# Packet sizes and issue times of loads and stores in a DMA-bound weight-normalised matmul

## The chip, the cores and the metric

The kernel runs on one core of one Trainium2 chip. The metric is the device time of one execution in microseconds (us), lower is better, as the median of several executions. The span of a profile is about 1.3 us shorter than the time measured for the same execution.

## The reference

```
W_adapted = W + scale * (lora_A @ lora_B)                  # 256 x 256
W_final   = W_adapted / sqrt(sum(W_adapted ** 2, axis=0) + 1e-8) * m
y         = x.reshape(-1, 256) @ W_final                   # x: 32768 x 256, float32
```

The weights are tiny. What counts is that x (33.6 MB) is read once and y (33.6 MB) is written once.

## The kernel before

x is cut into 8 blocks of 4 MB. Each block has 8 chunks, and each chunk is 4 rows of 1 KB on each of 128 partitions. The kernel keeps 5 blocks in the on-chip memory, and the results overwrite x in place. Blocks 0 to 2 must be stored before blocks 5 to 7 can be loaded. SP, an engine that here only issues transfers, issues the loads (queue q1 in the profile), and ACT, one of the compute engines, the stores (q10).

```
    loads = [(0, 2), (2, 2), (4, CH - 4)] + units[1 : XBUFS - 1]      # (first chunk, chunks)
    loads += [((XBUFS - 1) * CH, CH - 3)]
    loads += [(XBUFS * CH - 3 + c, 1) for c in range(3)] + units[XBUFS:]
    ...
    stores = [(b * CH, CH, 21 + b) for b in range(F - 1)]             # (..., issue after chunk)
    stores += [(G - CH, CH // 2, 24), (G - CH // 2, CH // 2, 24)]
    FIRST = len(stores)
    stores += [(G + c, 1, G + 3) for c in range(4)]
    stores += [(G + 4, CH - 4, 47)]
    stores += [(b * CH, CH, max(47, (b + 1) * CH - 1)) for b in range(F + 1, NBLK - 1)]
    stores += [(g0, cnt, g0 + cnt - 1) for g0, cnt in units[-2:]]
    HALF = FIRST - 2
    ...
        if loads[n][0] == XBUFS * CH:          # block 5 waits for blocks 0, 1 and half of 2
            for k in range(HALF + 1):
                nc.sync.wait_ge(sem(f"store{k}"), 16)
```

Here CH = 8 (chunks in a block), F = 3 and G = 24. One transfer of n rows per partition leaves 128 packets of n KB in the trace, which is 8 on each of the 16 DMA engines. The size of a transfer in rows is therefore also its packet size. The rest of a chunk's way is a cast to bf16 on POOL, transposes on PE (the matrix engine), a copy on VectorE, the product on PE, and a copy back on ACT.

Of the kernel before, what the change touches and what calls it, by code (L numbers as in the profile page):

```python
# [11 lines left out]
def kernel(  # L12
# [10 lines left out]
    nc = tc.nc  # L23
# [6 lines left out]
    x_flat = x.flatten_outer_dims()  # L30
    out_flat = out.flatten_outer_dims()
# [4 lines left out]
    J = 4  # L36
    DJ = 32
    BLK = DJ * P
    NBLK = N // BLK
# [3 lines left out]
    XBUFS = 5  # L43
    CH = DJ // J
    NCH = NBLK * CH

    NPR = NCH // 2
# [1 line left out]
    NXB = 2  # L49

    REST = 15
    IDLE = 8
    NXT = 2
    F8 = 2 * J * P

# [7 lines left out]
    def sb(name, shape, dtype):  # L63
        return ctx.enter_context(nc.sbuf_tensor(name, shape, dtype))
# [4 lines left out]
    x_bufs = [sb(f"x_sb{k}", [P, DJ, IN], FP32) for k in range(XBUFS)]  # L69
    xb_bufs = [sb(f"xb{k}", [P, 2 * J, IN], BF16) for k in range(NXB)]  # L70
# [4 lines left out]
    m_row = sb("m_row", [1, OUT], FP32)  # L75
    identity = sb("identity", [P, P], FP32)
    zeros = sb("zeros", [P, P], FP32)
    ones = sb("ones", [P, P], FP32)
# [18 lines left out]
    mb_ps = y_ps[1][:, 2, :]  # L97
# [3 lines left out]

    units = [(b * CH, CH) for b in range(NBLK - 1)]
    units += [(NCH - CH, CH // 2), (NCH - CH // 2, CH // 2)]
    loads = [(0, 2), (2, 2), (4, CH - 4)] + units[1 : XBUFS - 1]


    loads += [((XBUFS - 1) * CH, CH - 3)]
    loads += [(XBUFS * CH - 3 + c, 1) for c in range(3)] + units[XBUFS:]
    load_of = {g: n for n, (g0, cnt) in enumerate(loads) for g in range(g0, g0 + cnt)}




    F = NBLK - XBUFS
    G = F * CH
    stores = [(b * CH, CH, 21 + b) for b in range(F - 1)]
    stores += [(G - CH, CH // 2, 24), (G - CH // 2, CH // 2, 24)]
    FIRST = len(stores)
    stores += [(G + c, 1, G + 3) for c in range(4)]
    stores += [(G + 4, CH - 4, 47)]  # L120
    stores += [(b * CH, CH, max(47, (b + 1) * CH - 1)) for b in range(F + 1, NBLK - 1)]
    stores += [(g0, cnt, g0 + cnt - 1) for g0, cnt in units[-2:]]
    HALF = FIRST - 2


    late = [nc.alloc_semaphore(f"store{n}") for n in range(FIRST, len(stores))]
    sems = {f"store{FIRST + k}": s for k, s in enumerate(late)}

    def sem(name):
        if name not in sems:  # L130
            sems[name] = tc.alloc_semaphore(name)
        return sems[name]

    def in_sbuf(g0, cnt):
        b, c = divmod(g0, CH)
        return x_bufs[b % XBUFS][:, c * J : (c + cnt) * J, :]

    def in_dram(dram, g0, cnt):
        (u0, ucnt), = [u for u in units if u[0] <= g0 < u[0] + u[1]]
        unit = dram[u0 * J * P : (u0 + ucnt) * J * P].rearrange("(p j) k -> p j k", p=P)  # L140
        return unit[:, (g0 - u0) * J : (g0 - u0 + cnt) * J, :]

    def load_x(n):
        nc.sync.dma_start(
            out=in_sbuf(*loads[n]), in_=in_dram(x_flat, *loads[n])
        ).then_inc(sem(f"load{n}"), 16)

    def store_y(n):
        nc.scalar.dma_start(
            out=in_dram(out_flat, *stores[n][:2]), in_=in_sbuf(*stores[n][:2])  # L150
        ).then_inc(sem(f"store{n}"), 16)


    nc.sync.dma_start(
        out=w_nat[:], in_=W.rearrange("(p t) o -> p t o", t=KC)
    ).then_inc(sem("load_w"), 16)
    nc.scalar.dma_start(
        out=a_nat[:], in_=lora_A.rearrange("(p t) r -> p t r", t=KC)
# [1 line left out]
    nc.scalar.dma_start(out=b_nat[:], in_=lora_B).then_inc(sem("load_b"), 16)  # L160
    nc.scalar.dma_start(out=m_row[:], in_=m[None, :]).then_inc(sem("load_m"), 16)
    for n in range(len(loads)):
        if loads[n][0] == XBUFS * CH:


            for k in range(HALF + 1):
                nc.sync.wait_ge(sem(f"store{k}"), 16)
        if loads[n] == units[-1]:
            nc.sync.wait_ge(sem(f"store{HALF + 1}"), 16)
        load_x(n)  # L170


# [3 lines left out]
        out=identity[:],  # L176
        in_=zeros[:],
# [3 lines left out]
        pattern=[[-1, P]],  # L181
        channel_multiplier=1,
    ).then_inc(sem("ident"), 1)
    for p in range(NPR):
        b, c = divmod(p, PRB)
        for g in (2 * p, 2 * p + 1):
            if g == 0 or load_of[g - 1] != load_of[g]:
                nc.gpsimd.wait_ge(sem(f"load{load_of[g]}"), 16)
        if p == 0:


            nc.gpsimd.wait_ge(sem("dve"), 4)
        if p == REST:
            nc.gpsimd.wait_ge(sem(f"store{HALF}"), 16)
        if p >= NXB:
            nc.gpsimd.wait_ge(sem("turned"), p - NXB + 1)
        nc.gpsimd.tensor_copy(  # L197
            out=xb_bufs[p % NXB][:],
            in_=x_bufs[b % XBUFS][:, 2 * c * J : 2 * (c + 1) * J, :],
        ).then_inc(sem("rounded"), 1)  # L200

    nc.gpsimd.wait_ge(sem("turned"), NPR - NXB + 1)
    nc.gpsimd.memset(xb_bufs[NPR % NXB][:], 0.0).then_inc(sem("rounded"), 1)  # L203


    for _ in range(IDLE):
        nc.gpsimd.wait_ge(sem("ident"), 1)


    dv = sem("dve")  # L210
    nc.vector.memset(ones[:], 1.0)
# [8 lines left out]
        out=wa[:], in0=ab_ps, scalar=float(scale), in1=w_nat[:], op0=ALU.mult, op1=ALU.add  # L220
    ).then_inc(dv, 1)
    nc.vector.wait_ge(dv, 3)
    nc.vector.tensor_mul(out=sq[:], in0=wa[:], in1=wa[:]).then_inc(dv, 1)  # L223
    nc.vector.wait_ge(sem("pe"), 4)
    nc.vector.tensor_copy(out=m_all[:], in_=mb_ps).then_inc(dv, 1)  # L225
    nc.vector.wait_ge(dv, 5)
    for t in range(KC):
# [5 lines left out]
    for t in range(KC):  # L233
        i = nc.vector.tensor_mul(out=w_final[:, t], in0=wam[:, t], in1=rnorm[:])  # L234
    i.then_inc(dv, 1)
    for p in range(NPR):
        nc.vector.wait_ge(sem("turned"), p + 1)
        nc.vector.tensor_copy(  # L238
            out=xt_bufs[p % NXT][:].rearrange("p r t -> p (r t)").bitcast(FP32),
            in_=xt_ps[p % 2][:],  # L240
        ).then_inc(sem("copied"), 1)


    nc.scalar.wait_ge(dv, 1)

    nc.scalar.activation(out=warm[:], in_=eps_col[:], func=AF.Sqrt)  # L246
    nc.scalar.wait_ge(sem("pe"), 3)
    nc.scalar.activation(  # L248
        out=norm[:], in_=n2_ps, func=AF.Sqrt, bias=eps_col[:]
    ).then_inc(sem("act"), 1)  # L250
    drains = 0
    for g in range(NCH):
        b, c = divmod(g, CH)
        nc.scalar.wait_ge(sem("product"), g + 1)

        nc.scalar.copy(  # L256
            out=x_bufs[b % XBUFS][:, c * J : (c + 1) * J, :], in_=y_ps[g % 2][:]
        ).then_inc(sem("room"), 1)
        due = [n for n in range(len(stores)) if stores[n][2] == g]
        if due:  # L260
            drains += 1
            nc.scalar.drain().then_inc(sem("done"), 1)  # L262
            nc.scalar.wait_ge(sem("done"), drains)
            for n in due:
                store_y(n)


    pe = sem("pe")
# [6 lines left out]
    for t in range(KC):  # L275
        i = nc.tensor.matmul(  # L276
            ab_ps[:, t, :], aT[:, t * P : (t + 1) * P], b_bf[:], start=True, stop=True
        )
    i.then_inc(pe, 1)
    nc.tensor.wait_ge(dv, 4)  # L280

    for t in range(KC):
# [1 line left out]
            n2_ps, ones[:], sq[:, t, :], start=(t == 0), stop=(t == KC - 1)  # L284
        )
    i.then_inc(pe, 1)
    nc.tensor.wait_ge(sem("load_m"), 16)
    nc.tensor.matmul(mb_ps, ones[0:1, :], m_row[:], start=True, stop=True).then_inc(pe, 1)  # L288
    def take(name):

        nc.tensor.sem_inc(sem(name), -1).wait_op(sem(name), 1, "sem-ge")  # L291
# [4 lines left out]
        j_order.append(a + J // 2)  # L296

    def turned(p):
        take("rounded")

        for j in range(2 * J):
            i = nc.tensor.transpose(  # L302
                xt_ps[p % 2][:, j * P : (j + 1) * P],
                xb_bufs[p % NXB][:, j, :].bitcast(FP32),
                identity[:],
            )
        i.then_inc(sem("turned"), 1)

    def product(p):
        take("copied")  # L310
        for h in range(2):
            take("room")
            for t in range(KC):
                for j in j_order:
                    r = (h * J + j) * P
                    i = nc.tensor.matmul(  # L316
                        y_ps[h][:, j, :],
                        xt_bufs[p % NXT][:, r : r + P, t],
                        w_final[:, t, :],
                        start=(t == 0 and (j % (J // 2)) == 0),  # L320
                        stop=(t == KC - 1 and (j % (J // 2)) == (J // 2) - 1),
                    )
            i.then_inc(sem("product"), 1)

    turned(0)

    nc.tensor.wait_ge(dv, 8)
    nc.tensor.sem_inc(sem("room"), 2)
    with nc.Fori(0, NPR // 2, 1, engines=[PE], head_slot={PE: 128}):
        turned(1)  # L330
        product(0)
        turned(0)
        product(1)

# [1 line left out]
    critical.close()  # L336
    tc.close()
    tc.compile()
    for s in late:
        nc.sync.wait_ge(s, 16)  # L340
        nc.sync.sem_clear(s)


# [33 lines left out]
```

## Time and profile before

| | before |
|---|---|
| median time, 3 executions | 162.48 us (162.4 to 162.73) |
| span of the profile | 161.3 us |
| bytes moved | 67.42 MB, 418 GB/s over the span |
| PE busy | 59% |
| last store issued | 132.23 us |

The DMA engines are busy from the second of the 40 slices to the last but one, so the bytes set the time. The question for any change is how much engine time is wasted. The prediction shows the lines.

The trace has a record of each DMA packet with its queue, bytes, start and duration. **Time lost up to t** is t minus (bytes moved by then) / 432.2 GB/s. That is the rate of 16 engines with 32 KB packets at their median of 1213 ns, and about what the trace holds for long (430 to 433). While the engines run at that rate, the number stands still. Where it grows, engine time is being wasted.

### The profile page before, as it was taken

To read this page: it belongs to the slowest core of one execution; us is meant where nothing else is said; L and a number is where in the kernel's file an instruction comes from. 1 tells how busy PE (TensorE), PEld (TensorE's weight loads), DVE (VectorE), ACT (ScalarE), POOL (GpSimd) and SP (SyncE) were. 2 spreads that over 40 slices of the span, in tenths; PEclk is the share of its full clock that TensorE was granted. 3 is DMA by queue.
4 is the path that set the end of the run, shared out by engine and by line. 5 is a ranking of instruction groups with operands and counts; after the bars stand their busy time and mean duration, and the time that the engine had idled before them with its cause. 6 is when DMAs were issued, how large, how long until landed. Compare 5 with 4: busy or idle time off the path is not lost. (4 is left out here: it accounts for less than half of the span.)

```text
span 161.3 us, 2012 instructions
## 1 busy us (share of the span) xinstructions
PE 95.2 (59%) x786; PEld 83.8 (52%) x786; DVE 46.6 (29%) x44; ACT 63.9 (40%) x67; POOL 62.9 (39%) x39
## 2 busy tenths in 40 slices
PE   0491899999999700000199999999999940000000
PEld 0160799999998600000179989989899930000000
DVE  0439635353635300000033535353445300000000
ACT  3010076868686520000027675856776850000000
POOL 1085339776764000000674479198676200000000
PEclk9999999999999995555559999999999998555555
DMA  4999999999899999989999999999999999999995
GB/s 163 427 455 459 390 504 406 390 488 423 374 412 361 511 423 390 473 374 451 427 482 414 386 463 421 407 433 433 422 484 419 406 479 414 400 479 423 386 443 228
DMA packets 4356, 67.42 MB, mean 418 GB/s; under 512 B 625, under 2 KB 642, under 8 KB 1666
## 3 DMA queue, kind: packets, MB, share of 16 engines
q1 hardware_dynamic: 2160, 33.82, 49.5%
q10 hardware_dynamic: 2194, 33.59, 48.7%
q14 instruction: 2, 0.02, 0.0%
HBM read 33.85 MB, written 33.55 MB: 418 GB/s over the span
## 5 line engine op out<-in xcount | busy, mean ns | idle before, releaser
L256 ACT COPY x_sb<-y_ps 128x1024 f32<-128x1024 f32 x64 | 62.0, 1014 | 60.0 <-PE y_ps L316 57.8
L197 POOL CAST xb<-x_sb 128x2048 bf16<-128x2048 f32 x32 | 60.4, 1900 | 61.3 <-DMA out_dram<-x_sb 27.7
L316 PE MATMUL y_ps<-w_final,xt 128*128 128x256 bf16 x512 | 63.6, 278 | 1.2 <-PEq L291 1.1
L238 DVE COPY xt<-xt_ps 128x1024 f32<-128x1024 f32 x32 | 39.2, 1224 | 72.6 <-PE xt_ps L302 72.6
L316 PEld LDWEIGHTS y_ps<-w_final,xt 128*128 128x128 bf16 x512 | 51.1, 100 | 8.5 <-issue 1.9
L302 PE MATMUL xt_ps<-identity,xb 128*128 128x128 f32 x264 | 37.0, 287 | 28.2 <-PEq L291 28.2
L302 PEld LDWEIGHTS xt_ps<-identity,xb 128*128 128x128 f32 x264 | 31.7, 148 | 30.3 <-issue 30.0
L283 PE MATMUL y_ps<-sq,ones 128*128 128x256 f32 x4 | 2.1, 674 | 1.6 <-DVE sq L223 1.6
L272 PE MATMUL y_ps<-identity,a_nat 128*16 128x128 f32 x2 | 0.6, 394 | 4.1 <-DMA a_nat<-in_lora_A_dram 4.1
L248 ACT ACTIVATE norm<-y_ps,eps_col 128x256 f32<-128x256 f32 x1 | 0.5, 473 | 5.8 <-PE y_ps L283 5.8
L234 DVE TENSOR_TENSOR w_final<-wam,rnorm 128x256 bf16<-128x256 f32 x2 | 2.5, 1266 | 0.0
L283 PEld LDWEIGHTS y_ps<-sq,ones 128*128 128x128 f32 x4 | 1.2, 326 | 2.3 <-DVE sq L223 2.1
L272 PEld LDWEIGHTS y_ps<-identity,a_nat 128*16 128x16 f32 x2 | 0.1, 88 | 4.1 <-issue 4.1
L246 ACT ACT_TABLE_LOAD x1 | 1.3, 1283 | 2.4 <-issue 2.4
L203 POOL MEMSET xb<- 128x2048 bf16 x1 | 1.8, 1804 | 0.7 <-PE xt_ps L302 0.7
L231 DVE RECIPROCAL rnorm<-norm 128x256 f32<-128x256 f32 x1 | 1.7, 1747 | 0.0
L225 DVE COPY m_all<-y_ps 128x256 f32<-128x256 f32 x1 | 0.4, 424 | 3.3 <-PE y_ps L288 3.3
L214 DVE CAST b_bf<-b_nat 16x256 bf16<-16x256 f32 x1 | 0.3, 281 | 3.5 <-DMA b_nat<-in_lora_B_dram 3.5
L288 PE MATMUL y_ps<-m_row,ones 1*128 1x256 f32 x2 | 1.2, 706 | 0.0
L276 PE MATMUL y_ps<-b_bf,aT 16*128 16x256 bf16 x2 | 0.6, 404 | 0.7 <-DVE aT L216 0.7
L219 DVE SCALAR_TENSOR_TENSOR wa<-y_ps,w_nat 128x512 f32<-128x512 f32 x1 | 0.7, 692 | 0.8 <-PE y_ps L276 0.8
L288 PEld LDWEIGHTS y_ps<-m_row,ones 1*128 1x128 f32 x2 | 0.5, 308 | 0.6 <-issue 0.6
(13 smaller groups left out, 3.3 us busy)
## 6 DMA issues: line engine op xcount, KB each, us to landing
x_sb<-in_x_dram SPq DMA_DIRECT2D x5, 4096.0 KB, 26.5
out_dram<-x_sb ACTq DMA_DIRECT2D x5, 4096.0 KB, 22.7
out_dram<-x_sb ACTq DMA_DIRECT2D x5, 2048.0 KB, 29.0
x_sb<-in_x_dram SPq DMA_DIRECT2D x3, 2048.0 KB, 31.4
x_sb<-in_x_dram SPq DMA_DIRECT2D x1, 2560.0 KB, 44.8
x_sb<-in_x_dram SPq DMA_DIRECT2D x2, 1024.0 KB, 6.1
out_dram<-x_sb ACTq DMA_DIRECT2D x4, 512.0 KB, 50.1
x_sb<-in_x_dram SPq DMA_DIRECT2D x3, 512.0 KB, 46.4
```

What stands on the lines that cost most here:

```text
L197: nc.gpsimd.tensor_copy(out=xb_bufs[p % NXB][:], in_=x_bufs[b % XBUFS][:, 2 * c * J : 2 * (c + 1) * J, :],).then_inc(sem("rounded"), 1)
L203: nc.gpsimd.memset(xb_bufs[NPR % NXB][:], 0.0).then_inc(sem("rounded"), 1)
L219: nc.vector.scalar_tensor_tensor(out=wa[:], in0=ab_ps, scalar=float(scale), in1=w_nat[:], op0=ALU.mult, op1=ALU.add).then_inc(dv, 1)
L231: nc.vector.reciprocal(out=rnorm[:], in_=norm[:]).then_inc(dv, 1)
L234: i = nc.vector.tensor_mul(out=w_final[:, t], in0=wam[:, t], in1=rnorm[:])
L238: nc.vector.tensor_copy(out=xt_bufs[p % NXT][:].rearrange("p r t -> p (r t)").bitcast(FP32), in_=xt_ps[p % 2][:],).then_inc(sem("copied"), 1)
L246: nc.scalar.activation(out=warm[:], in_=eps_col[:], func=AF.Sqrt)
L256: nc.scalar.copy(out=x_bufs[b % XBUFS][:, c * J : (c + 1) * J, :], in_=y_ps[g % 2][:]).then_inc(sem("room"), 1)
L283: i = nc.tensor.matmul(n2_ps, ones[:], sq[:, t, :], start=(t == 0), stop=(t == KC - 1))
L288: nc.tensor.matmul(mb_ps, ones[0:1, :], m_row[:], start=True, stop=True).then_inc(pe, 1)
L302: i = nc.tensor.transpose(xt_ps[p % 2][:, j * P : (j + 1) * P], xb_bufs[p % NXB][:, j, :].bitcast(FP32), identity[:],)
L316: i = nc.tensor.matmul(y_ps[h][:, j, :], xt_bufs[p % NXT][:, r : r + P, t], w_final[:, t, :], start=(t == 0 and (j % (J // 2)) == 0), stop ...
```

## The change

The intent was to smooth the changes of direction between loads and stores. A first small store opens the store queue early, beside large loads. Small loads keep the load queue alive while large stores run. Chunks arrive in half blocks, so that compute starts sooner. The core of the diff, with cuts marked by "...":

```
-    loads = [(0, 2), (2, 2), (4, CH - 4)] + units[1 : XBUFS - 1]
...
-    stores = [(b * CH, CH, 21 + b) for b in range(F - 1)]
-    stores += [(G - CH, CH // 2, 24), (G - CH // 2, CH // 2, 24)]
+    H = XBUFS * CH
+    loads = [(0, 2, 2 * J), (2, 2, 2 * J)] + [(g0, 4, 4 * J) for g0 in range(4, 24, 4)]
+    loads += [(24, CH, CH * J), (H - CH, 4, 4 * J), (H - 4, 4, J)]
+    loads += [(b * CH, CH, CH * J) for b in range(XBUFS, NBLK - 1)]
+    loads += [(g0, cnt, cnt * J) for g0, cnt in units[-2:]]
...
+    stores = [(0, 1, J, 13), (1, CH - 1, (CH - 1) * J, 20), (CH, CH, CH * J, 21)]
+    stores += [(G - CH, 2, 2 * J, G - 1), (G - 6, 6, 6 * J, G - 1)]
     FIRST = len(stores)
-    stores += [(G + c, 1, G + 3) for c in range(4)]
-    stores += [(G + 4, CH - 4, 47)]
...
+    stores += [(G, 4, J, G + 3), (G + 4, CH - 4, (CH - 4) * J, 48)]
+    stores += [(b * CH, CH, CH * J, max(48, (b + 1) * CH - 1)) for b in range(F + 1, NBLK - 1)]
...
+    wait_load(nc.scalar, 0)                       # ACT casts pair 0, POOL starts at pair 1
+    nc.scalar.copy(out=xb_bufs[0][:], in_=x_bufs[0][:, 0 : 2 * J, :]).then_inc(
+        sem("early"), 1
+    )
```

The third number is now the rows of one transfer (J = 4), and the fourth of a store is the chunk after which it is issued. The rest of the diff reorders the setup: the product for m comes ahead of that for the norm, POOL waits for the weights, and idle waits are moved.

More of the change, by code (lines that the diff above doesn't have):

```diff
@@ L51 @@
     REST = 15
-    IDLE = 8
     NXT = 2
@@ L103, with pieces @@
     units += [(NCH - CH, CH // 2), (NCH - CH // 2, CH // 2)]
-    loads = [(0, 2), (2, 2), (4, CH - 4)] + units[1 : XBUFS - 1]
-    loads += [((XBUFS - 1) * CH, CH - 3)]
-    loads += [(XBUFS * CH - 3 + c, 1) for c in range(3)] + units[XBUFS:]
-    load_of = {g: n for n, (g0, cnt) in enumerate(loads) for g in range(g0, g0 + cnt)}
     F = NBLK - XBUFS
     G = F * CH
-    stores = [(b * CH, CH, 21 + b) for b in range(F - 1)]
-    stores += [(G - CH, CH // 2, 24), (G - CH // 2, CH // 2, 24)]
-    FIRST = len(stores)
-    stores += [(G + c, 1, G + 3) for c in range(4)]
-    stores += [(G + 4, CH - 4, 47)]
-    stores += [(b * CH, CH, max(47, (b + 1) * CH - 1)) for b in range(F + 1, NBLK - 1)]
-    stores += [(g0, cnt, g0 + cnt - 1) for g0, cnt in units[-2:]]
-    HALF = FIRST - 2
+    H = XBUFS * CH
[3 more added lines that the diff above has]
+    loads += [(g0, cnt, cnt * J) for g0, cnt in units[-2:]]
+    load_of = {g: n for n, (g0, cnt, _) in enumerate(loads) for g in range(g0, g0 + cnt)}
+    stores = [(0, 1, J, 13), (1, CH - 1, (CH - 1) * J, 20), (CH, CH, CH * J, 21)]
+    stores += [(G - CH, 2, 2 * J, G - 1), (G - 6, 6, 6 * J, G - 1)]
+    FIRST = len(stores)
+    stores += [(G, 4, J, G + 3), (G + 4, CH - 4, (CH - 4) * J, 48)]
+    stores += [(b * CH, CH, CH * J, max(48, (b + 1) * CH - 1)) for b in range(F + 1, NBLK - 1)]
+    stores += [(g0, cnt, cnt * J, g0 + cnt - 1) for g0, cnt in units[-2:]]
+    def pieces(entry):
+        return 16 * (entry[1] * J // entry[2])
     late = [nc.alloc_semaphore(f"store{n}") for n in range(FIRST, len(stores))]
@@ L132, in sem, with transfer, wait_load, wait_store @@
         return sems[name]
-    def in_sbuf(g0, cnt):
+    def transfer(engine, name, entry, dram, store):
+        g0, cnt, rows = entry[:3]
         b, c = divmod(g0, CH)
-        return x_bufs[b % XBUFS][:, c * J : (c + cnt) * J, :]
-    def in_dram(dram, g0, cnt):
         (u0, ucnt), = [u for u in units if u[0] <= g0 < u[0] + u[1]]
         unit = dram[u0 * J * P : (u0 + ucnt) * J * P].rearrange("(p j) k -> p j k", p=P)
-        return unit[:, (g0 - u0) * J : (g0 - u0 + cnt) * J, :]
+        for r in range(0, cnt * J, rows):
+            here = x_bufs[b % XBUFS][:, c * J + r : c * J + r + rows, :]
+            there = unit[:, (g0 - u0) * J + r : (g0 - u0) * J + r + rows, :]
+            src, dst = (here, there) if store else (there, here)
+            engine.dma_start(out=dst, in_=src).then_inc(sem(name), 16)
     def load_x(n):
-        nc.sync.dma_start(
-            out=in_sbuf(*loads[n]), in_=in_dram(x_flat, *loads[n])
-        ).then_inc(sem(f"load{n}"), 16)
+        transfer(nc.sync, f"load{n}", loads[n], x_flat, False)
     def store_y(n):
-        nc.scalar.dma_start(
-            out=in_dram(out_flat, *stores[n][:2]), in_=in_sbuf(*stores[n][:2])
-        ).then_inc(sem(f"store{n}"), 16)
+        transfer(nc.scalar, f"store{n}", stores[n], out_flat, True)
+    def wait_load(engine, g):
+        engine.wait_ge(sem(f"load{load_of[g]}"), pieces(loads[load_of[g]]))
+    def wait_store(engine, n):
+        engine.wait_ge(sem(f"store{n}"), pieces(stores[n]))
     nc.sync.dma_start(
@@ L162 @@
     for n in range(len(loads)):
-        if loads[n][0] == XBUFS * CH:
-            for k in range(HALF + 1):
-                nc.sync.wait_ge(sem(f"store{k}"), 16)
-        if loads[n] == units[-1]:
-            nc.sync.wait_ge(sem(f"store{HALF + 1}"), 16)
+        if loads[n][0] == H:
+            for k in range(FIRST - 1):
+                wait_store(nc.sync, k)
+        if loads[n][0] == H + G - CH:
+            wait_store(nc.sync, FIRST - 1)
         load_x(n)
@@ L183 @@
     ).then_inc(sem("ident"), 1)
-    for p in range(NPR):
+    for p in range(1, NPR):
         b, c = divmod(p, PRB)
         for g in (2 * p, 2 * p + 1):
-            if g == 0 or load_of[g - 1] != load_of[g]:
-                nc.gpsimd.wait_ge(sem(f"load{load_of[g]}"), 16)
-        if p == 0:
-            nc.gpsimd.wait_ge(sem("dve"), 4)
+            if g == 2 or load_of[g - 1] != load_of[g]:
+                wait_load(nc.gpsimd, g)
+        if p == 1:
+            nc.gpsimd.wait_ge(sem("dve"), 6)
+        if p == 2:
+            nc.gpsimd.wait_ge(sem("dve"), 8)
         if p == REST:
-            nc.gpsimd.wait_ge(sem(f"store{HALF}"), 16)
+            wait_store(nc.gpsimd, FIRST - 2)
         if p >= NXB:
@@ L203 @@
     nc.gpsimd.memset(xb_bufs[NPR % NXB][:], 0.0).then_inc(sem("rounded"), 1)
-    for _ in range(IDLE):
-        nc.gpsimd.wait_ge(sem("ident"), 1)
     dv = sem("dve")
@@ L223 @@
     nc.vector.tensor_mul(out=sq[:], in0=wa[:], in1=wa[:]).then_inc(dv, 1)
-    nc.vector.wait_ge(sem("pe"), 4)
+    nc.vector.wait_ge(sem("pe"), 3)
     nc.vector.tensor_copy(out=m_all[:], in_=mb_ps).then_inc(dv, 1)
@@ L235 @@
     i.then_inc(dv, 1)
+    nc.vector.wait_ge(dv, 8)
+    nc.vector.sem_inc(sem("room"), 2)
     for p in range(NPR):
@@ L241 @@
         ).then_inc(sem("copied"), 1)
+    for engine, idle in ((nc.gpsimd, 8), (nc.vector, 24)):
+        for _ in range(idle):
+            engine.wait_ge(sem("ident"), 1)
     nc.scalar.wait_ge(dv, 1)
     nc.scalar.activation(out=warm[:], in_=eps_col[:], func=AF.Sqrt)
-    nc.scalar.wait_ge(sem("pe"), 3)
+    wait_load(nc.scalar, 0)
+    nc.scalar.copy(out=xb_bufs[0][:], in_=x_bufs[0][:, 0 : 2 * J, :]).then_inc(
+        sem("early"), 1
+    )
+    nc.scalar.wait_ge(sem("pe"), 4)
     nc.scalar.activation(
@@ L258 @@
         ).then_inc(sem("room"), 1)
-        due = [n for n in range(len(stores)) if stores[n][2] == g]
+        due = [n for n in range(len(stores)) if stores[n][3] == g]
         if due:
@@ L279 @@
     i.then_inc(pe, 1)
+    nc.tensor.wait_ge(sem("load_m"), 16)
+    nc.tensor.matmul(mb_ps, ones[0:1, :], m_row[:], start=True, stop=True).then_inc(pe, 1)
     nc.tensor.wait_ge(dv, 4)
@@ L286 @@
     i.then_inc(pe, 1)
-    nc.tensor.wait_ge(sem("load_m"), 16)
-    nc.tensor.matmul(mb_ps, ones[0:1, :], m_row[:], start=True, stop=True).then_inc(pe, 1)
     def take(name):
@@ L298, in turned @@
     def turned(p):
-        take("rounded")
         for j in range(2 * J):
@@ L323, in product @@
             i.then_inc(sem("product"), 1)
+    nc.tensor.wait_ge(sem("early"), 1)
     turned(0)
-    nc.tensor.wait_ge(dv, 8)
-    nc.tensor.sem_inc(sem("room"), 2)
     with nc.Fori(0, NPR // 2, 1, engines=[PE], head_slot={PE: 128}):
+        take("rounded")
         turned(1)
         product(0)
+        take("rounded")
         turned(0)
@@ L338 @@
     tc.compile()
-    for s in late:
-        nc.sync.wait_ge(s, 16)
+    for k, s in enumerate(late):
+        nc.sync.wait_ge(s, pieces(stores[FIRST + k]))
         nc.sync.sem_clear(s)
```

## The prediction

> **What bounds the kernel now.** I read the page's part 2 first, because 67 MB in 161 us on one core suggests the DMA engines, then the chain, the table of windows, the timeline around each change of direction, and last the trace's packet records (queue, bytes, start and duration of each packet), which the page only sums.
>
> ```profile
> DMA  4999999999899999989999999999999999999995
> GB/s 163 427 455 459 390 504 406 390 488 423 374 412 361 511 423 390 473 374 451 427 482 414 386 463 421 407 433 433 422 484 419 406 479 414 400 479 423 386 443 228
> DMA packets 4356, 67.42 MB, mean 418 GB/s; under 512 B 625, under 2 KB 642, under 8 KB 1666
> ```
>
> The DMA row is full from the second slice to the last but one. The swings of the GB/s row are an artefact: a packet's bytes are booked where it starts, and 32 KB packets start in waves. Compute is not the limit: PE is 59% busy, and the chain of waits covers only 113 to 132 us.
>
> ```profile
> PE 10%; ACT 1%; ACTq 1%; issue 0%
> ```
>
> It ends in the ACT queue, which issues the last store at 132.23 us; from there to 161.3 us only stores drain.
>
> ```profile
> 4.50:48.50 44.00, 37.56 (x294) 32.63 (x294) 22.16 (x23) 21.67 (x23) 26.84 (x15) 1.00 1.00 430
> 48.50:50.50 2.00, 2.00 (x21) 1.88 (x19) 0.97 (x1) 1.01 (x1) 1.67 (x1) 1.00 1.03 412
> 50.50:52.50 2.00, 1.90 (x18) 1.50 (x17) 1.22 (x1) 1.77 (x2) 0.00 (x0) 1.00 1.01 305
> ...
> 82.50:115.00 32.50, 31.66 (x276) 28.26 (x275) 14.09 (x12) 21.88 (x23) 21.75 (x12) 0.97 1.00 426
> 117.00:159.00 42.00, 14.03 (x129) 12.78 (x126) 5.34 (x5) 11.56 (x12) 6.73 (x4) 0.73 1.01 433
> ```
>
> This is the table by windows; its last two columns are DMA share and GB/s. Loads alone run at 430, stores alone at 433, the mixture at 426 or more. Only one place is slow with the engines still "busy": 50.5 to 52.5 us at 305. There the loads end in 4 KB packets and the first store, issued at 48.53, is about to enter. That place costs 2.0 x (1 - 305/432) = 0.59 us, and the two microseconds before it (412) 0.09.
>
> ```profile
> 48.53 0.37 ACTq L149 DMA_DIRECT2D out_dram<-x_sb  x1
> ...
> 77.92 7.48 SPq L144 DMA_DIRECT2D x_sb<-in_x_dram  x4
> ...
> 110.85 1.30 ACTq L149 DMA_DIRECT2D out_dram<-x_sb  x3
> ...
> 132.23 0.34 ACTq L149 DMA_DIRECT2D out_dram<-x_sb  x1
> ```
>
> These timeline lines are the three changes of direction and the last issue. By the packet records the first store packet starts at 52.6 (4.1 us after issue), the first resumed load at 81.6 (3.7 us after). At both the engines stay fed; there is no idle hole to close, only slow packets at the first.
>
> **What the skill says.** (1) "DMA: Bandwidth & Descriptors", section "Where 436 GB/s comes from": the 16 ports give 435.2 GB/s. The trace agrees: 430 to 433. At 432 the 67.42 MB take 156.1 us, and span 161.3 less 156.1 leaves 5.2 us for start, tail and slow packets together. (2) Same page, "Queues, rings and completion order": each engine takes queues in turn, a whole packet at a time. The trace agrees: with 32 KB loads beside 4 KB stores (84 to 100 us) the packet records give 380 to 385 against 47 to 51 GB/s, eight to one. (3) Same page, "Why small descriptors are slow (HBM only)": a fixed cost per packet. The records agree: median 1213 ns for 32 KB, 611 for 16 KB, 309 for 8 KB, 159 for 4 KB, where an eighth of 1213 is 152. (4) "SBUF — State Buffer", section "SBUF: two separate sides": VectorE with two SBUF inputs and GpSimd exclude each other. The trace agrees in kind: the final weight product takes 1266 ns each while POOL casts, the same shape 421 ns in the product before it.
>
> **The change part by part.** Engine time is the currency: a packet costs its duration on one of 16 engines, and a 128-partition transfer puts 8 packets on each.
>
> *Bytes*: unchanged, so 156 us of the span cannot move.
>
> *Blocks 1 and 2 in half loads*: 8 packets of 32 KB per engine become 16 of 16 KB per block. By the medians, 16 x 611 - 8 x 1213 = 72 ns a block, 0.14 us for two. Their gain is that chunks reach POOL earlier: POOL now idles 2.78 us before block 1 and 1.42 before block 2. That is compute time, off the DMA path.
>
> *Last half of block 4 and first chunk of stores*: before, 3 loads and 4 stores of one chunk in 4 KB packets; after, 4 loads and 5 stores. Two more at 8 x (159 - 152) = 56 ns: +0.11 us. The store packets otherwise keep their number (28 and 24 KB cost what 32 KB does per byte).
>
> *First change of direction*: the store queue is now opened by 8 small packets per engine beside large loads. Chunk 21 was ready at 48.5, and a pair of chunks takes 2.62 us, so chunk 13 would have been ready at 38; with the earlier start below, about 33 to 35, and at the old latency its packets flow from about 37. They pair with 8 large load packets per engine and end near 46, when the 28 KB rest of block 0 (due at chunk 20, about 43) follows in the same queue. The loads' 32 small packets per engine then alternate with about 28 to 32 store packets (8 each of 28, 32, 8 and 24 KB). So the state that was slow, small loads alone with a store about to enter, should vanish: -0.59 - 0.09 = -0.68 us. The records hold one hint that small loads between large stores run clean: two stragglers at 53.9 took 159 ns each.
>
> *Loads resumed at 2 chunks of block 2*: the store waited for lands near 73, so block 5 is issued some 5 us sooner. But it queues behind the small loads, which last as long as these stores: sum of the store packets 8 x (1.06 + 1.21 + 0.31 + 0.91) = 27.9 us, plus 32 x 0.16 = 5.1 us. Large loads start at about 82 as now. What it buys is a queue that never runs empty: records of 81.5 to 83 us show 418 to 427, worth 0.04 us.
>
> *Setup and ACT*: the m product goes ahead of the norm product, ACT casts pair 0, POOL waits for the weight products. Products can begin at about 14 us in place of 18.6. All of it beside loads; on the end it is worth 0, because the end is the last store, limited by bytes.
>
> *Stores after loads, at chunk 48 in place of 47*: block 6 should land at about 104.5 (before: 104.8). The new mark needs one more transpose group, product and ACT copy, some 2 us: issue at about 113 in place of 110.85. With 3.7 us latency the large stores arrive at about 116.6, just when loads end (116). A hole of 0 to 1 us is possible; I book +0.15.
>
> Sum: 0.14 + 0.11 - 0.68 - 0.04 + 0.15 = -0.32 us. The engines also end raggedly now (last store packets finish between 159.3 and 160.8); smoother changes could take a few tenths from that. I predict **162.0 us**.
>
> **The rivals.** (A) *A slow trickle.* The 50.5 to 52.5 packets averaged 216 ns in place of 159. If that is how a 4 KB load behaves whenever a store is active, and not just at a first entry, the 32 per engine would lose 32 x 57 = 1.8 us: about 164. For it: that window. Against: the two stragglers, and the 512 small stores beside large loads, mean 160 ns. (B) *A hole at the second change of direction*: the late mark at chunk 48 leaves the engines empty for 1 to 2 us near 116: 163 to 164. For it: my margin is about nil. Against: the store queue still has small packets until about then, and before, large stores followed them without a break (first at 115.8). (C) *A clean sweep*: all packets at median (the records' excess is 1.2 us in all) and an even finish (0.7 us): about 161. (D) *Compute becomes the bound*, since chunks 36 to 39 now arrive only at about 82: against it, block 5 comes at 93, and its four pairs before it need 2.62 us each; the last issue at 132 leaves 28 us of slack. No change.
>
> **Range and chances.** A gain of 2% would need 3.25 us; start, tail and slow packets together are 5.2 us, of which the change touches about 1.5. So faster by over 2% is nearly excluded. Slower by over 2% needs A and B together, or a stall I did not see. Range 161.1 to 163.0: C at the low end, half of A or B at the high end. Chances: faster 0.01, same 0.95, slower 0.04.
>
> **What would show it.** Right: no window near 46 to 54 us under 425 GB/s; both queues in flight from about 46 to 82 at 428 or more; 4 KB loads near 159 ns; block 5 issued near 73 but its packets not before 80; first product near 14 us; span near 160.8. Wrong: small loads at 200 ns or more in the long mixture (A), a DMA share under 0.95 near 113 to 118 (B), or POOL or SP waits that push the last issue from 132 to beyond 150. A time under 161 would mean that I undervalued the ragged finish; one above 163 that one of A and B is real.

## The result

| | before | after |
|---|---|---|
| median time, 6 executions each | 162.44 us (162.37 to 162.73) | 163.58 us (163.32 to 163.65) |
| span of the profile | 161.3 us | 162.0 us |
| last store: first and last of 16 engines landed | 159.83, 161.24 | 160.07, 161.98 |

The ratio is 1.0064, with a 95% interval of 1.0051 to 1.0077. Ratios here are the mean time of one kernel's fast runs over that of the other's of the same rounds, so not quite the ratio of the medians that I quote. The change is slower by about 1.1 us. That is within 2%, but it is outside my range of 161.1 to 163.0. The profiled execution of the changed kernel is its fastest (163.32), so the two profiles differ by only 0.7 us.

Part 2 of the page of the changed kernel, the same rows that the prediction shows of the kernel before:

```profile
DMA  4999999999898999999999999999999999999994
GB/s 164 427 449 421 429 445 417 429 502 421 356 401 386 431 437 434 427 418 433 436 467 421 437 445 421 391 435 435 426 477 404 461 429 396 463 423 413 421 417 206
DMA packets 4933, 67.43 MB, mean 416 GB/s; under 512 B 689, under 2 KB 706, under 8 KB 1986
```

The engines are as full as before. The swings of the GB/s row are smaller, because the packets are; slices 11 to 13 (40.5 to 52.6 us) read low, at 356, 401 and 386. The chain of waits (part 4) still ends in the issue of the last store, so the end is still bytes:

```profile
PE 11%; ACT 1%; ACTq 1%; issue 0%
```

The changed kernel in the table by windows (start and end, length, busy time of PE, PE loads, VectorE, ACT and POOL, clock, DMA share, GB/s):

```profile
44.50:46.50 2.00, 0.55 (x3) 0.58 (x4) 0.00 (x0) 0.00 (x0) 2.00 (x2) 0.81 1.00 295
54.00:68.00 14.00, 1.78 (x16) 1.25 (x14) 1.07 (x1) 2.53 (x3) 0.00 (x0) 0.69 1.02 436
```

The first line is the finding. From 44.5 to 46.5 us, with a DMA share of 1.00, the engines move 295 GB/s. This is the same picture as 50.5 to 52.5 us before (305 GB/s), six microseconds earlier. There the slow packets were 4 KB loads; here they are 16 KB loads. The second line is the long mixture of 4 KB loads and large stores that I had feared. It runs at full rate, and the 512 small loads take 159 ns each, their undisturbed duration.

The issues of the changed kernel in the timeline:

```profile
32.98 0.37 ACTq L145 DMA_DIRECT2D out_dram<-x_sb  x1
...
42.55 0.37 ACTq L145 DMA_DIRECT2D out_dram<-x_sb  x1
...
44.08 0.34 ACTq L145 DMA_DIRECT2D out_dram<-x_sb  x1
...
74.26 9.26 SPq L145 DMA_DIRECT2D x_sb<-in_x_dram  x4
...
114.81 3.97 ACTq L145 DMA_DIRECT2D out_dram<-x_sb  x3
...
139.60 0.34 ACTq L145 DMA_DIRECT2D out_dram<-x_sb  x1
```

The small opener goes out at 32.98 and the first large store at 42.55, six microseconds sooner than before (48.53). In the packet records the large store's packets start at 46.6, 4.1 us after its issue, exactly the delay of before. Between 2.1 and 4.1 us after the issue the loads are slow. So the stretch is tied to the issue of the first large store, and it moved with it.

Time lost, worked out from the packet records as defined above:

```
time lost (us) up to      34     44     50     56     84    116    156
before                  2.69   2.70   2.80   3.42   3.46   3.61   3.65
after                   2.76   2.87   3.60   3.61   3.79   3.89   3.97
```

From 34 to 56 us the kernel before loses 0.73 and the changed one 0.85. Of this difference 0.10 falls before 44 us, where the opener enters; from 44 to 56 it is 0.72 against 0.74. So in this pair of profiles the stretch has moved and kept its size. From 56 to 84 it is 0.04 against 0.18, and after that the two are equal. By 156 us the changed kernel is 0.32 us behind on average over the engines. The last store adds to this: its first engine lands 0.24 us later, its last one 0.74 us later. The engines finish over 1.91 us in place of 1.41.

### The profile page after: what moved, and what is told of

Its sections match the earlier page's. It is cut to its first block, busy times and chain, and to the rows that moved or that the text cites. A ratio compares the mean times of both kernels' runs of the same rounds, so it can differ in the third digit from the quotient of the medians.

```text
span 162.0 us, 2028 instructions
## 1 busy us (share of the span) xinstructions
PE 98.2 (61%) x786; PEld 86.3 (53%) x786; DVE 45.1 (28%) x44; ACT 65.7 (41%) x68; POOL 60.8 (38%) x38
## 5 line engine op out<-in xcount | busy, mean ns | idle before, releaser
L205 POOL CAST xb<-x_sb 128x2048 bf16<-128x2048 f32 x31 | 58.3, 1896 | 70.8 <-DMA x_sb<-in_x_dram 34.2
L332 PE MATMUL y_ps<-w_final,xt 128*128 128x256 bf16 x512 | 64.6, 281 | 5.6 <-PEq L308 5.5
L332 PEld LDWEIGHTS y_ps<-w_final,xt 128*128 128x128 bf16 x512 | 51.7, 101 | 13.5 <-issue 6.2
L318 PE MATMUL xt_ps<-identity,xb 128*128 128x128 f32 x264 | 38.9, 297 | 29.7 <-PEq L308 29.7
L318 PEld LDWEIGHTS xt_ps<-identity,xb 128*128 128x128 f32 x264 | 33.6, 154 | 31.5 <-issue 31.1
L261 ACT CAST xb<-x_sb 128x2048 bf16<-128x2048 f32 x1 | 1.9, 1899 | 2.6 <-DMA x_sb<-in_x_dram 2.6
L232 DVE TENSOR_TENSOR wam<-wa,m_all 128x256 f32<-128x256 f32 x2 | 0.8, 422 | 0.0
```

The lines of the kernel that those rows point to most:

```text
L205: nc.gpsimd.tensor_copy(out=xb_bufs[p % NXB][:], in_=x_bufs[b % XBUFS][:, 2 * c * J : 2 * (c + 1) * J, :],).then_inc(sem("rounded"), 1)
L261: nc.scalar.copy(out=xb_bufs[0][:], in_=x_bufs[0][:, 0 : 2 * J, :]).then_inc(sem("early"), 1)
L318: i = nc.tensor.transpose(xt_ps[p % 2][:, j * P : (j + 1) * P], xb_bufs[p % NXB][:, j, :].bitcast(FP32), identity[:],)
L332: i = nc.tensor.matmul(y_ps[h][:, j, :], xt_bufs[p % NXT][:, r : r + P, t], w_final[:, t, :], start=(t == 0 and (j % (J // 2)) == 0), stop ...
```

## The experiments

Each kernel was timed in five rounds against the kernel before on the same chip, and all results were correct. The kernel before had medians of 162.49 to 162.55 in these rounds. A summary comes first. "Issue" is that of the first store larger than 4 KB per packet. "Lost" is the time lost between 1.5 and 5 us after it. "Loads" are the load packets that started 1.8 to 4.5 us after it, with their mean duration and the undisturbed one. "Finish" is the time between the first and the last engine of the last store. All but the median and the ratio come from the one profiled execution.

```
                              issue   lost   loads: KB, mean ns (undisturbed)  finish  median   ratio
before                        48.53   0.62    4   207  (159)                    1.41   162.44   1
after                         42.55   0.72   16   919  (611)                    1.91   163.58   1.0064
no early store                42.97   1.08   16   963  (611)                    2.13   163.46   1.0054
block 2 as 4 and 4            42.76   0.81   16   871  (611)                    1.86   163.43   1.0054
second large store at 23      43.00   0.95   16   919  (611)                    2.10   163.30   1.0049
before, block 0 at 17         44.14   1.02   20  1155  (764)                    1.73   163.20   1.0042
no idle waits on VectorE      44.36   0.93   16   934  (611)                    1.74   163.82   1.0076
block 0 in 7 KB packets       44.54   0.84   16   892  (611)                    1.90   163.47   1.0050
22, no opener                 48.24   0.65    4   205  (159)                    1.58   162.72   1.0015
whole loads                   48.84   0.69    4   206  (159)                    1.59   162.96   1.0022
large stores at 22            48.97   0.40    4   185  (159)                    1.61   162.86   1.0021
setup only                    49.61   0.07    4   164  (159)                    1.39   162.62   1.0017
before, 22 and 48             49.69   0.06    4   164  (159)                    1.70   163.06   1.0026
resume after six, 47          49.71   0.06    4   164  (159)                    1.73   162.82   1.0026
resume after six, 48          49.91   0.05    4   164  (159)                    0.87   163.59   1.0055
before, 23                    51.04   0.00   none                               1.27   164.27   1.0117
22 and whole loads            51.46   0.03    4   160  (159)                    1.46   162.70   1.0017
```

Three groups stand out. Issued before 45 us, the first large store costs the loads 0.7 to 1.1 us, and the kernel takes 163.2 to 163.8. Issued between 48.2 and 49 us, it costs 0.4 to 0.7 us. Issued after 49.6 us, with the loads ending near 52 to 53, it costs nearly nothing. The time does not follow all the way: the third group takes 162.62 to 164.27, and none of it is shown faster than the kernel before.

**Setup only.** The changed kernel's program with the old lists of loads and stores (abridged, the comments are mine):

```
+    loads = [(0, 2, 2 * J), (2, 2, 2 * J), (4, 4, 4 * J)] + ...   # as before
+    stores = [(0, CH, CH * J, 21), (CH, CH, CH * J, 22)] + ...    # as before, 47 for 48
```

> The changed kernel's setup (cast of pair 0 on ACT, m product early, POOL gated by the weight products, idle waits moved to POOL and VectorE) with the loads and stores of the kernel before. Theory 1 (the whole loss sits in the new order and sizes of loads and stores): as fast as before, 162.4 within 0.2, first product near 14 us, the slow stretch before the first store at 0.6 us as before. Rival (the setup or the shifted instruction fetches on the DMA engines cost something at the ragged finish): 162.7 to 163.0.

It ran at 162.62 (162.25 to 163.72), ratio 1.0017 with an interval of 0.9992 to 1.0041: not told apart from the kernel before. By itself the setup is not the cause. Against my expectation the stretch at 51 us nearly vanished, because its first store happened to be issued at 49.61, later than before (48.53) in spite of the earlier first product. In its place 0.16 us was lost near 81 and 0.4 near 115.

```profile
49.61 0.37 ACTq L146 DMA_DIRECT2D out_dram<-x_sb  x1
```

**No early store.** The changed kernel with block 0 whole:

```
-    stores = [(0, 1, J, 13), (1, CH - 1, (CH - 1) * J, 20), (CH, CH, CH * J, 21)]
+    stores = [(0, CH, CH * J, 20), (CH, CH, CH * J, 21)]
```

> The changed kernel, but block 0 stored whole in 32 KB packets at chunk 20, no early 4 KB store. Theory (the slow stretch comes whenever the first large store packets enter behind a deep stock of committed loads, and a 4 KB opener does nothing against it): the stretch is as long as in the changed kernel, about 0.7 to 0.8 us, and the time is equal or up to 0.2 us better (163.3 to 163.6). Rival (the opener does halve the loss, as it was meant to): the stretch grows and the time is 163.8 or more.

The time is 163.46 (163.09 to 163.76), not told apart from the changed kernel. The profiled execution, its slowest, lost 1.08 us in the stretch in place of 0.72. So the opener may shorten the stretch somewhat, but the time gains nothing from it.

**Block 2 as 4 and 4.** The changed kernel with `(G - CH, 4, 4 * J, G - 1), (G - 4, 4, 4 * J, G - 1)` for the 2 and 6 chunks.

> The changed kernel with block 2 stored in two halves of 4 chunks (16 KB packets) in place of 2 and 6 chunks, loads resumed after the first 4. Theory (the 8 KB packets paired with 4 KB loads lose about 0.1 us between 66 and 84 us): 0.1 us better than the changed kernel, 163.4 to 163.5. Rival (the resume point sets how ragged the engines become): 0.3 us or more better.

163.43 (163.08 to 163.76): the resume point is not the cause. Its profile loses 0.15 us from 66 to 84 us where the changed kernel loses 0.16, so the 8 KB packets are not the cause of that loss either.

**Before, 23.** The kernel before with the first two stores issued later:

```
-    stores = [(b * CH, CH, 21 + b) for b in range(F - 1)]
+    stores = [(b * CH, CH, 23) for b in range(F - 1)]
```

> The kernel before, with blocks 0 and 1 stored at chunk 23 in place of 21 and 22, so that the first large store is issued near 51.2 us, when only about 1 us of loads is left. Theory (the slow stretch of 0.6 us is large store packets read ahead while some 4 us of loads are committed before them; with few loads left there is nothing to slow): the stretch at 305 GB/s vanishes, the first store packet starts near 52.5, time 161.8 to 162.2. Rival (the first large store of a run costs its 0.6 us wherever it stands, or needs 4 us from issue to first packet): engines idle for 1 to 3 us near 53, time 163 to 165.

The half of the theory about the stretch held: it is gone, and the first store packet starts 1.1 us after its issue with no hole. The half about the time failed: 164.27 (163.18 to 164.54). The profile lost 1.0 us when the loads came back near 81 us, where this time the stores slowed (from 74 to 84 us those of 4 KB took 282 ns on average in place of 159), 0.3 more up to 116 us and 0.2 after. Even this was its fastest execution. Why this kernel pays at the return and the kernel before does not (0.04) was not found.

**Whole loads.** The changed kernel with blocks 1 and 2 in one load each: `(8, 8, 8 * J), (16, 8, 8 * J)` for the four half loads.

> The changed kernel with blocks 1 and 2 loaded whole, in 32 KB packets. By the packet records the halves cost 0.08 us of engine time up to 34 us. Theory: 0.1 us better than the changed kernel if chunk 13 and the stores come at the same time; but compute then waits for whole blocks, the first stores come later, when fewer loads are left, and the slow stretch shrinks with it: 0.2 to 0.5 us better, 163.1 to 163.4. Rival (the stretch does not depend on when the store is issued): 0.1 better and no more.

162.96, which is 0.6 better than the changed kernel and more than I expected. Compute now waits for whole blocks, and with the same setup and the same marks the first large store is issued at 48.84 in place of 42.55:

```profile
48.84 0.37 ACTq L145 DMA_DIRECT2D out_dram<-x_sb  x1
```

The half loads themselves cost 0.04 us of engine time up to 34 us (2.76 against 2.72).

**No idle waits on VectorE.** `(nc.vector, 24)` becomes `(nc.vector, 0)`.

> The changed kernel without the 24 idle waits on VectorE. Every run with the new setup shows an additional 8 KB instruction packet just as ACT issues its last store, and at that instant one DMA engine's store packets are 0.35 to 0.5 us over their median; the spread of the last stores over the engines grows there from about 1.3 to 1.9 us. Theory: the idle waits decide whether that packet exists; without them it goes or moves, and the time falls by 0.2 to 0.5 us if it goes. Rival: the packet belongs to ACT's own longer program; nothing changes.

The additional instruction packet went, but the time did not improve: 163.82 (163.37 to 164.64). That theory fell.

**Block 0 in 7 KB packets.** `(1, CH - 1, (CH - 1) * J, 20)` becomes `(1, CH - 1, CH - 1, 20)`.

> The changed kernel with the 7 chunks of block 0 stored in four transfers of 7 KB packets in place of one of 28 KB. Theory (the loss at the entry of stores is data of large packets read ahead of their turn, so it grows with the packet that enters): the stretch near 45 us shrinks from 0.7 to 0.3 us or less, and the smaller packets cost 0.2 to 0.3: equal to the changed kernel within 0.2, with the loss moved. Rival (the loss comes with the change of direction and not with packet size): the stretch stays at 0.7 and the time rises by 0.2 to 0.3.

The stretch stayed (0.84), so it is not a matter of the entering packet's size, and that theory fell too. The time, 163.47, did not rise by the 0.2 to 0.3 that the rival gave it.

**Before, 22 and 48.** The kernel before with `22` for `21 + b` and `48` for `47`.

> The kernel before with the first two stores at chunk 22 (issue near 50, with about 2 us of loads left) and the stores after the loads at chunk 48 in place of 47. Theory (a store issued at most 2 us before the loads end meets no slow stretch): the stretch near 51 falls from 0.45 to under 0.1 us, that near 115 from 0.1 to under 0.05, time 161.8 to 162.2, if the return to loads near 80 us stays as smooth as before; the run at chunk 23 lost 1 us there, and I do not know why, so 163 is possible.

The profile is the best of all in engine time: 3.21 us lost by 156 us, 0.44 less than before. But that execution (162.40) was the fastest of six, and the median is 163.06, well above the 161.8 to 162.2 that I expected. What the others lost was not seen.

**Large stores at 22.** The changed kernel, nothing touched but when its two large stores go out:

```
-    stores = [(0, 1, J, 13), (1, CH - 1, (CH - 1) * J, 20), (CH, CH, CH * J, 21)]
+    stores = [(0, 1, J, 13), (1, CH - 1, (CH - 1) * J, 22), (CH, CH, CH * J, 22)]
```

> The changed kernel with its first two large stores issued at chunk 22 in place of 20 and 21, near 50 us, when only the 4 KB loads are left; nothing else touched. Theory (the stretch stands 2.1 to 4.1 us after the issue of the first large store, and only where loads still flow there): it shrinks from 0.7 to 0.3 us or less and the time falls by 0.3 to 0.6, to 163.0 to 163.3, unless the return of the loads, which then meets an empty load queue, takes some back. Rival (the small loads or the opener themselves cause the stretch): 0.7 us stay, time 163.5.

Its timeline, the opener and then both large stores at once:

```profile
34.69 0.37 ACTq L145 DMA_DIRECT2D out_dram<-x_sb  x1
48.97 0.85 ACTq L145 DMA_DIRECT2D out_dram<-x_sb  x2
```

162.86 (162.62 to 163.07): 0.7 us of the 1.1 came back by issuing the same stores later. The stretch costs 0.40 in place of 0.72. The engines are 0.20 us less behind at 156 us, and they finish over 1.61 us in place of 1.91.

**Second large store at 23.** The changed kernel with `(CH, CH, CH * J, 23)`.

> The changed kernel with the second large store (block 1) issued at chunk 23 in place of 21, some 9 us after the first. In all runs with a slow stretch so far two large stores were issued 1.5 us apart just before it. Theory (the first large store alone sets it): the stretch still begins 2.1 to 2.5 us after the first large store's issue and costs 0.7 us, time within 0.1 of the changed kernel. Rival (the second issue while the first is being taken up causes it): no stretch near 45 us, time 0.5 to 0.7 better.

```profile
43.00 0.37 ACTq L145 DMA_DIRECT2D out_dram<-x_sb  x1
...
52.01 1.36 ACTq L145 DMA_DIRECT2D out_dram<-x_sb  x3
```

The two large stores are now 9 us apart, and the stretch still follows the first one and costs 0.95. The first store alone sets it. The time, 163.30 (163.15 to 163.85), overlaps the changed kernel's.

**Resume after six.** A version meant to beat both: the kernel before with 22, block 2 as `(G - CH, 6, 24), (G - 2, 2, 24)`, and 48.

> A version meant to beat both: the kernel before with the first two stores at chunk 22, the stores after the loads at chunk 48, and block 2 stored as 6 and 2 chunks with the loads resumed after the 6. Theory (a transfer that enters an idle queue slows the other direction from 2 to 4 us after its issue, as long as large packets of the other direction are still flowing): all three changes of direction now have at most 2.5 us of the other direction left at issue; losses at 51, 81 and 115 us together under 0.2 us where the kernel before has 0.7; time 161.7 to 162.1. Rival (the loss at the return to loads is not tied to how much of the stores is left): time 162.5 to 163.5 as with chunks 22 and 48 alone.

163.59 (162.77 to 164.52). The stretch is gone, but the profiled execution, the slowest, has a hole at the other change of direction. Its timeline and its table by windows:

```profile
117.13 1.82 ACTq L149 DMA_DIRECT2D out_dram<-x_sb  x3
```

```profile
117.00:119.00 2.00, 1.59 (x15) 1.23 (x13) 1.23 (x1) 0.03 (x2) 1.21 (x2) 1.00 0.62 262
```

The stores were issued just as the loads ended (the last load packet at 117.19), the first store packet came at 117.97, and the DMA share falls to 0.62. So issuing late has its own price as soon as it is too late. The same version with 47 in place of 48:

> As the version that resumes after six chunks, but with the stores after the loads at chunk 47, 2 us sooner, because at chunk 48 they came at 117.1 us, after the loads had ended, and left a hole of 2 us. Theory: the hole goes; issue near 115, time 161.8 to 162.4. Rival (the return to the loads costs 0.3 us or more in most executions wherever it stands): 162.5 to 163.

The hole is gone, and the time is 162.82 (162.49 to 163.32), inside the rival's range and still not better than the kernel before. Its profile lost 3.29 us by 156 us where the kernel before lost 3.65, but its last engine lands 0.10 us sooner only, at 161.14. The finish takes 1.73 us in place of 1.41.

**22, no opener** and **22 and whole loads.** The changed kernel with `(0, CH, CH * J, 22), (CH, CH, CH * J, 22)`, and the changed kernel with the opener, 22 and whole loads.

> The changed kernel with blocks 0 and 1 stored whole at chunk 22 and no 4 KB opener. Against the changed kernel with chunk 22 and the opener (162.86): if the opener's loss at 40 to 44 us (0.17) is its own, 0.1 to 0.2 better, 162.65 to 162.75; if the loss has to do with the half loads or the finish, equal within 0.1.

> The changed kernel with chunk 22 and with blocks 1 and 2 loaded whole. Against the changed kernel with chunk 22 alone (162.86): the half loads' 0.1 us is saved, 162.7 to 162.8; if compute now comes so late that the first large store is issued after the loads end, a hole, 163 or more.

162.72 (162.62 to 163.0) and 162.70 (162.52 to 163.53). Each is some 0.15 better than 22 alone, as expected, but that is no more than the scatter. Neither is below the kernel before.

**Before, block 0 at 17.** The converse test. The kernel before with nothing changed but one issue time:

```
-    stores = [(b * CH, CH, 21 + b) for b in range(F - 1)]
+    stores = [(b * CH, CH, 17 + 5 * b) for b in range(F - 1)]
```

> The kernel before with nothing changed but block 0 stored at chunk 17 in place of 21, near 43 us, when some 9 us of loads are left. Theory (loads slow from 2.1 to 4.1 us after the issue of the first large store, as far as they still flow): the slow stretch moves to about 45 to 47 us, fills its whole 2 us and costs 0.7 to 1.0 in place of 0.5; time 162.7 to 163.1. Rival (the loss in the changed kernel needs its half loads, its opener or its setup): the loss stays at 0.5, time 162.5, or falls because the stores now alternate with loads early.

```profile
44.14 0.37 ACTq L149 DMA_DIRECT2D out_dram<-x_sb  x1
51.09 0.37 ACTq L149 DMA_DIRECT2D out_dram<-x_sb  x1
```

163.20 (163.09 to 163.48) against 162.50, ratio 1.0042 with an interval of 1.0013 to 1.0071. The loss appears in the kernel before, without half loads, opener or new setup, by issuing its first store 4.4 us sooner. Loads of 20 KB took 1155 ns in place of 764, and 3.96 us were lost by 156 us, as in the changed kernel (3.97).

## Why the prediction was wrong

The step that failed is this one: "So the state that was slow, small loads alone with a store about to enter, should vanish: -0.59 - 0.09 = -0.68 us." I had seen the slow stretch once, and named it by two things that happened to stand there: small loads, and a store queue not yet opened. Neither is needed. It came back with 16 KB and 20 KB loads, and behind an opener that was already flowing: its packets ran from 37.3 to 45.15, as predicted, and the large store issued at 42.55 still had its first packet only at 46.63. What the runs show in its place is that the loads are slow from about 2.1 to 4.1 us after the first large store is issued, as far as loads are still flowing then. Before, the issue at 48.53 left loads worth about 1.5 us for that window (149 packets of 159 ns on 16 engines); the change moved it to 42.55, with more loads than the window could hold. The term measured +0.12 us (34 to 56 us: 0.85 against 0.73) where I had -0.68: nothing was saved at the stretch, and the opener's entry added 0.10.

This holds for the first change of direction, and not as it stands for the second. There the kernel before issued large stores at 110.85, with loads flowing until 117.4 and small stores in the queue, and lost only 0.08 us from 112 to 118; the setup alone, issued at 110.43 in the same situation, lost 0.34. Why one paid and the other did not is open.

The other terms of the sum, against the time-lost table:

- Half loads: +0.14 predicted, +0.07 seen up to 34 us. Right in kind, half the size.
- Two more one-chunk transfers: +0.11 predicted. Their 4 KB packets took the 159 ns that the sum was made with.
- Loads resumed earlier, queue never empty: -0.04 predicted, +0.14 seen from 56 to 84 us. The wait and the order were right: block 5 was issued at 74.26 and its packets started at 82.9. Time was lost there that I had not counted. 8 KB stores are not the reason (16 KB in their place lost as much). The kernel with whole loads, whose small loads ended at 62.6 in place of 83.4 us, lost 0.02 there; but the changed kernel with chunk 22, whose small loads ended at 62.5, lost 0.13, most of it from 80 to 82 us. The cause is open.
- Stores after the loads at chunk 48: +0.15 predicted, nothing seen. The issue at 114.81 had its first packet at 116.0, after 1.2 us and not 3.7, with few loads left (they ended at 116.98). Rival B did not occur here. It did in the version with the hole.
- Setup: worth 0 predicted, and 162.62 measured for the setup alone. The first product moved as I said, from 18.60 to 14.16:

```profile
18.60 2.54 PE L316 MATMUL y_ps<-w_final,xt 128*128 128x256 bf16 x16
```

```profile
14.16 1.91 PE L332 MATMUL y_ps<-w_final,xt 128*128 128x256 bf16 x16 [1.83 <-PEq L308]
```

The prediction took this for harmless, and the setup alone bears it out. What brought chunk 20 to 42.5 us is the half loads: with whole loads, the same setup and the same marks it came at 48.8. What the earlier setup adds to that was not tested. The prediction had called the half loads' gain compute time, off the DMA path; through the issue of the store it was not.

- Rival A, small loads that crawl beside stores, is refuted: 512 of them at 159 ns.
- The finish: I hoped for a few tenths, and the spread of the last store over the engines grew from 1.41 to 1.91 us.

The issue time is shown as the main cause from both sides: issued later in the changed kernel it gave back 0.7 of 1.1 us, and issued sooner in the kernel before it cost 0.7. The time lost in the engines is less than half of that (0.20 and 0.31 us by 156 us). The rest goes with a wider finish, which all kernels with the first large store before 45 us have (1.73 to 2.13 us). That the slow stretch makes the engines uneven fits this, but it was not shown, and two kernels without a stretch came to 1.70 and 1.73 us too.

Open are what happens inside a DMA engine in those 2 us; why kernels without any stretch were still not faster than the kernel before; and the last 0.3 us of the changed kernel with chunk 22.

## What to carry to other kernels

In this kernel, where loads and stores share saturated DMA engines, the issue time of the first large transfer into the other direction turned out to be a tuning knob of its own: too early it cost 0.7 us, and the late issue at 117.13 left a hole. Compute that runs ahead can move that issue and make a byte-bound kernel slower, so when you speed up what comes before it, check whether the issue moved. And name a slow stretch by what it moves with, not by what stands beside it: one more run with a shifted issue would have corrected this prediction.

## What the Trainium skill lacked or had wrong

- "DMA: Bandwidth & Descriptors", section "Latency and other measured facts", gives about 0.6 us to the first byte for transfers issued from SP or ACT. Here the first load took 1.0 us from issue to first packet on idle engines, a store 4.1 us (48.53 to 52.63) with loads flowing, and 1.2 us (114.81 to 116.02) with few loads left.
- The same page, section "Queues, rings and completion order", has the turn by turn of packets, which the runs confirm, but nothing on the cost of starting the other direction: 16 KB loads took 919 ns on average in place of 611 between 1.8 and 4.5 us after the issue of the first large store.
- The same section calls 9 to 17 descriptors typical of a packet. The packet records here show one packet for each partition's contiguous run, up to 32 KB (1213 ns), and 32 KB loads beside 4 KB stores moved eight times as much (380 to 385 against 47 to 51 GB/s), so the turns are as coarse as the transfers are laid out.
- The same page, section "Why small descriptors are slow (HBM only)", works its fixed cost per packet out for 256 bytes only. Here 4 KB took 159 ns and an eighth of 32 KB 152, some 5%, while 16 KB (611) costs under 1% over half of 32 KB.
- No page has a figure for how unevenly saturated engines finish: the 16 engines of the last store landed over 1.41 us before and 1.91 us after.
